# Scratch of rotated queries and keys, laid out by head and row first

## The chip, the cores and the metric

The kernel runs on one core of a Trainium2 chip. The metric is the device time of one execution in microseconds, as the median over runs. The core has a matrix engine (TensorE, PE in the profile; its weight loads are a row of their own, PEld), a vector engine (VectorE, DVE), a scalar engine (ScalarE, ACT), a third elementwise engine (GpSimd, POOL) and SyncE (SP), which here only issues transfers. Sixteen DMA engines move data between the device memory (DRAM) and the on-chip memory of 128 partitions. Matrix products accumulate in PSUM.

## What is computed

One layer of a streaming encoder over 2048 frames of width 1024, in float32. Only the part in bold passes through the changed code; the rest is the work around it.

```
h = rms_norm(x, norm_gain)
q_a, k_a, v_a, g_a, q_r, k_r, v_r, g_r, m_a, m_r = split(h @ w_in)
o_a = chunk_band_attention(q_a, k_a, v_a, rel_bias)            # 8 heads of 64
branch_a = (o_a * silu(g_a)) @ w_out_attn
qr, kr = rotary(q_r), rotary(k_r)                              # 8 heads of 64 = 2 halves of 32
o_r = retention_chunkwise(qr, kr, v_r)                         # keys 64, values 128
branch_r = (groupnorm(o_r) * silu(g_r)) @ w_out_ret
out = rms_norm(x + (sigmoid(m_a)*branch_a + sigmoid(m_r)*branch_r) @ w_out, final_gain)
```

**The rotation and the retention** are what matters. `rotary` takes the first and the second 32 columns of each head, `x1` and `x2`, and gives `x1*cos - x2*sin` and `x1*sin + x2*cos`. Retention forms products of queries and keys over the 64 columns of a head, weights them with a decay, multiplies by the values, and adds the query times a running state (the decayed sum of key times value of all earlier frames). A sum over the 64 columns does not depend on their order, provided queries, keys and state agree on it.

## The kernel before, in words

Every float32 operand of a matrix product is kept as a high and a low part (`split`: a rounded copy on ACT, the rest by a subtraction on DVE or POOL), and a product is made of two or three matrix products of parts. The 2048 frames are four blocks of `B` = 512 frames, and a block is two units of `T` = 256.

The program is written in stages: the projections to q, k, v of blocks 0 and 1 (`p0`), then attention and retention on them, the projections of blocks 2 and 3 (`p1`), attention and retention on these, then the output products. The gate projections (`g0`, `g1`) and part of the output products (`ba`, `br`) are a stream of dense steps that `fill(n)` interleaves with attention and retention: PE gets some retention matmuls, then some steps of dense matmuls (three matmuls of 512 columns each), and so on, in a written order that PE keeps. `later` and `put` hang DVE, POOL and DMA work on the count of those steps. All transfers except one are issued by SP (`dma`), in the order in which the program writes them. In attention and retention ACT, DVE and POOL are put in order by a scheduler, PE and SP are not.

**From projection to retention.** `ep_rotated` rotates the two halves of a group of four heads (`cc` is the group, 0 or 1). `xs[0]` and `xs[1]` are tiles of 128 rows, row = 32 * head in group + frequency: `xs[0]` has the first halves, `xs[1]` the second halves of all four heads. `parted` splits both and stores high and low parts to scratch in DRAM, `qrscr` (line 171) for queries and `krscr` (line 170) for keys, each 256 KB store taking 128 rows of two units of 256 frames. `keys` (line 896) also turns the rotated keys by 8 PE transposes a group and block (`trkr`), 64 in all, makes the high and low parts, and stores them to `kdscr`, from which the state is formed.

**Retention.** `retention(s, ...)` runs over pairs (`p`, `st`): four pairs of heads, and four units of 256 frames for each. There are 16 pairs in a stage, each of two items `i` (one head). `load(p, st)` (line 1276) brings what a pair needs: the keys `ks` (`kr`) by two transfers, the queries of each head (`qr`) by two transfers a head, values (`vr`) by one a head, the turned keys `kd` by one. A query tile has 128 partitions: the 64 columns of the head (two halves of 32) twice over, since high and low keys both meet the same queries. A key tile has the 64 high rows above the 64 low rows. `scores` makes four matmuls of 256 columns into `sr` from `kr` and `qr`, DVE multiplies by the decay mask (line 1326), ACT and DVE split the result into `sh` and `sl`. `output` makes six matmuls with the values, and two with the state where there is one, into `o`; `update` makes four matmuls `kv` from `vr` and `kd`. `evacuate` copies `o` (ACT, line 1383), stores it, squares it on POOL (line 1390), and splits the square for four `ssq` matmuls. The scores of an item are formed two items ahead of its output, and a pair is loaded when the item three ahead belongs to it, that is, its load is written one item before its first scores and a whole pair before its first output. Its tiles come from a ring of 21 buffers (`e`), so a load also waits until the tile that was in its buffer is read out.

The lines that the change touches read in this way in the kernel before. `r` is the row of the head within its group, 32 rows a head.

```
krscr[cc][b]: [unit, part, half, 128 rows, 256 frames]
qrscr[cc][b]: [unit, half, 128 rows, part, 256 frames]
ks[:, i]               <- krscr[un, :, :, r:r + 32]      "n h c t -> (n h) c t"
q[64*half:64*half+64]  <- qrscr[un, :, r:r + 32]         "h c n t -> h c (n t)"
```

Of the kernel before, what the change touches and what calls it, by code (L numbers as in the profile page):

```python
# [12 lines left out]
F32R = mybir.dt.float32r  # L13
# [8 lines left out]
P = 128  # L22
# [7 lines left out]
NB = SEQ // B  # L30
T = 256
# [34 lines left out]
def hybrid_kernel(  # L66
# [30 lines left out]
    def r32(ap):  # L97
        return ap.bitcast(F32)
# [7 lines left out]
    def E(name, dt=F32, shape=(P, 512)):  # L106
        return epool[0].tile(list(shape), dt, tag="e", name=name)

    def TR(name):
        return xpool[0].tile([P, 512], F32, tag="tr", name=name)  # L110

    def D(name, shape, dt=F32):
        return dram.tile(list(shape), dt, name=name)
# [31 lines left out]
    pe, act, dve, pool = Ordered(nc.tensor), Sometimes(nc.scalar), Sometimes(nc.vector), Sometimes(nc.gpsimd)  # L145
# [21 lines left out]
    kascr = [[D(f"kas_{h}_{b}", [P, B], F32R) for b in range(NB)] for h in range(HEADS)]  # L167
    vascr = [[D(f"vas_{h}_{b}", [P, B], F32R) for b in range(NB)] for h in range(HEADS)]

    krscr = [[D(f"krs_{c}_{b}", [2, 2, 2, P, T], F32R) for b in range(NB)] for c in range(2)]  # L170
    qrscr = [[D(f"qrs_{c}_{b}", [2, 2, P, 2, T], F32R) for b in range(NB)] for c in range(2)]
    kdscr = [[D(f"kds_{p}_{b}", [P, 2, 2, T], F32R) for b in range(NB)] for p in range(4)]
    vrscr = [[D(f"vrs_{h}_{b}", [P, 4, 2, DV], F32R) for b in range(NB)] for h in range(HEADS)]
    uascr = [[D(f"uas_{p}_{b}", [P, B]) for b in range(NB)] for p in range(4)]
# [59 lines left out]
    def later(n, fn):  # L234

        order[0] += 1
        deferred.append((steps[0] + n, order[0], fn))
        deferred.sort(key=lambda e: e[:2])

    def put(lag, dst, src):  # L240

        later(lag, lambda: dma(dst, src))
# [522 lines left out]
    def halves(t):  # L765
        return r32(t).rearrange("p (u n) -> p u n", u=2)

    def two(name, shape=(P, 512)):
        return [E(f"{n}_{name}", F32R, shape) for n in "hl"]
# [75 lines left out]
    def ep_rotated(kind):  # L845

        def epilogue(cc, b, j, src, ps):
            a = plain(src, ps, f"x{kind}_{cc}_{b}_{j}")
            if (kind, cc, b) not in firsts:
                firsts[kind, cc, b] = j, a  # L850
                return
            j0, a0 = firsts.pop((kind, cc, b))
            xs = [a, a0] if j0 else [a0, a]
            c, s = tables.pop((kind, cc, b))
            nm = f"{kind}_{cc}_{b}"
            ts = [E(f"t{n}_{nm}") for n in range(2)]

            def cross():
                for n in range(2):
                    pool.tensor_tensor(ts[n], xs[1 - n], s, ALU.mult)  # L860

            def own(n):
                dve.tensor_tensor(xs[n], xs[n], c, ALU.mult)

            def both(n):
                dve.tensor_tensor(xs[n], xs[n], ts[n], ALU.add if n else ALU.subtract)

            later(3, cross)
            for n in range(2):
                later(7 + n, lambda n=n: own(n))  # L870
                later(9 + n, lambda n=n: both(n))
            (keys if kind == "k" else queries)(cc, b, xs, nm)

        return epilogue

    def parted(xs, nm, at, eng, dst):

        ws = {}

        def high(n):  # L880
            ws[n] = two(f"{nm}_{n}")
            act.copy(ws[n][0], xs[n])

        def low(n):
            eng.tensor_tensor(ws[n][1], xs[n], r32(ws[n][0]), ALU.subtract)
            for i in range(2):
                put(4, dst(i, n), halves(ws[n][i]))

        for n in range(2):
            later(at + n, lambda n=n: high(n))  # L890
            later(at + 4 + 2 * n, lambda n=n: low(n))

    def queries(cc, b, xs, nm):
        parted(xs, nm, 13, dve, lambda i, h: r32(qrscr[cc][b][:, h, :, i, :]).rearrange("u r t -> r u t"))

    def keys(cc, b, xs, nm):
        parted(xs, nm, 13, pool, lambda i, h: r32(krscr[cc][b][:, i, h]).rearrange("u r t -> r u t"))

        def turn(u):
            pk = TR(f"trkr_{nm}_{u}")  # L900
            v = pk.rearrange("p (t i h c) -> p t h i c", t=2, i=4, h=2)
            for t in range(2):
                for h in range(2):
                    pe.transpose(v[:, t, h], xs[h][:, (2 * u + t) * P:(2 * u + t + 1) * P], ident)
            pk = pk.rearrange("p (t i d) -> p i t d", t=2, i=4)
            kt = []

            def high(n):
                kt.append(E(f"kdt_{nm}_{u}_{n}", F32R, (P, 2, 2, P)))
                act.copy(kt[n][:, :, :, 0:HD], pk[:, 2 * n:2 * n + 2])  # L910

            def low(n):
                dve.tensor_tensor(
                    kt[n][:, :, :, HD:P], pk[:, 2 * n:2 * n + 2], r32(kt[n][:, :, :, 0:HD]), ALU.subtract
                )
                put(4, r32(kdscr[2 * cc + n][b][:, u]), r32(kt[n]).rearrange("p i t c -> p i (t c)"))

            for n in range(2):
                later(2 + n, lambda n=n: high(n))
                later(5 + n, lambda n=n: low(n))  # L920

        for u in range(2):
            later(15 + 4 * u, lambda u=u: turn(u))
# [344 lines left out]
    def retention(s, ps_ret):  # L1268
# [8 lines left out]
        def load(p, st):  # L1277
            b, un = st // 2, st % 2
            nm = f"{p}_{st}"
            cc = p // 2  # L1280
            ks = E(f"kr_{nm}", F32R, (P, 2, T))
            qs, vs = [], []
            for i in range(2):
                r = 32 * (2 * (p % 2) + i)
                dma(
                    r32(ks[:, i]),
                    r32(krscr[cc][b][un, :, :, r:r + 32]).rearrange("n h c t -> (n h) c t"),
                )
            for i in range(2):
                r = 32 * (2 * (p % 2) + i)  # L1290
                q = E(f"qr_{nm}_{i}", F32R, (P, 2, T))
                for half in range(2):
                    dma(
                        r32(q[64 * half:64 * half + 64]).rearrange("d n t -> d (n t)"),
                        r32(qrscr[cc][b][un, :, r:r + 32]).rearrange("h c n t -> h c (n t)"),
                    )
                qs.append(q)
                v = E(f"vr_{nm}_{i}", F32R, (P, 2, 2 * DV))
                dma(
                    r32(v), r32(vrscr[2 * p + i][b][:, 2 * un:2 * un + 2]).rearrange("p t n d -> p t (n d)")  # L1300
                )
                vs.append(v)
            kd = E(f"kd_{nm}", F32R, (P, 2, T))
            dma(r32(kd), r32(kdscr[p][b][:, un]))
            tiles[p, st] = ks, qs, vs, kd.rearrange("p i (t c) -> p i t c", t=2)
            if st == 4:
                sstk = epool[0].tile([P, 2, DV], F32R, tag="sstk", bufs=2, name=f"sstk_{p}_{st}")
                dma(r32(sstk).rearrange("p i c -> p (i c)"), r32(skscr[p]))
                sstks[p, 4] = sstk
# [98 lines left out]

        load_masks(0)
        load(*todo[0])  # L1410
        load(*todo[1])
        pend = None
        items = [(p, st, i) for p, st in todo for i in range(2)]
# [5 lines left out]
        for n, (p, st, i) in enumerate(items):  # L1419
            if i == 0:  # L1420
                ops = ps_ret.tile([P, 512], F32, tag="o", bufs=1, name=f"o_{p}_{st}")
            if i == 0 and st < 7:
                update(p, st)
            fill(RET_FILL)
            output(p, st, i, parts.pop((p, st, i)), ops)
            if i == 0 and pend:
                pend()
                pend = None
            if i == 1:
                pend = evacuate(p, st, ops)  # L1430
                tiles.pop((p, st))
            if n + 2 < len(items):
                parts[items[n + 2]] = scores(*items[n + 2])
            if i == 1 and n + 3 < len(items):
                p2, st2, _ = items[n + 3]
                if st2 == 4 * s:
                    load_masks(p2)
                load(p2, st2)
            fill(RET_FILL)
# [186 lines left out]
```

## Time and profile before

| | us |
|---|---|
| median of 3 runs | 2388.63 |
| lowest and highest of them | 2388.27 and 2393.96 |
| the profiled execution | 2389.42 |
| its span, first to last instruction | 2387.6 |
| PE busy in the span | 2031.1 |
| DVE, ACT, POOL busy | 1424.5, 874.8, 794.7 |
| mean busy share of the DMA engines' largest queue | 56.8% |

The profile is that of one execution. Its span is 1.8 us shorter than its own time, and that time is 0.8 us above the median. A row of a view of waits names the engine and what it was about to do, then after the arrow what ended the wait, the total in microseconds, the number of waits and the longest. A row of a view of windows gives for a stretch of the span the busy time of each engine with its number of instructions, then the mean TensorE clock that was granted (1.00 is full), the mean busy share of the 16 DMA engines and the bytes per time that they moved. A row of the view by tile gives the shortest, the median and the longest of a group's instructions. The name `qr<-qrs` is a transfer from the scratch of the queries into a query tile.

The stages stand in the span as follows: `p0` up to about 370 us, attention to 615, retention of blocks 0 and 1 from 615 to 972, `p1` to about 1320, attention to 1612, retention of blocks 2 and 3 from 1612 to 2016, and the output products to the end.

### The profile page before, as it was taken

The page shows a single profiled execution, that of the slowest core. Times are in us where ns is not written, and L with a number is a line of the kernel's source. Part 1 is how long each engine was busy: PE and PEld are TensorE (multiplying, and loading weights), DVE is VectorE, ACT ScalarE, POOL GpSimd, SP SyncE. Part 2 cuts the span into 40 slices and gives each one's busy share as a digit, 9 for nine tenths or more (in the row PEclk, how much of TensorE's full clock was granted, in tenths as well). Part 3 has the DMA queues.
Part 4 walks back from the last instruction along what each step waited for, and adds up shares of the span by engine and source line. Part 5 has one row for each costly group of instructions (what it writes and reads, how often), then busy time and mean ns, then how long its engine had stood idle before and what let it go on. Part 6 is the DMA issues. An engine that isn't in the chain of part 4 may idle for free. (4 is left out here: it accounts for less than half of the span.)

```text
span 2387.6 us, 30310 instructions
## 1 busy us (share of the span) xinstructions
PE 2031.1 (85%) x9744; PEld 1675.8 (70%) x9744; DVE 1424.5 (60%) x2491; ACT 874.8 (37%) x1727; POOL 794.7 (33%) x868
## 2 busy tenths in 40 slices
PE   5899899999867665899999999996766558999998
PEld 4687678888645554777777888884655447788887
DVE  7868686776434435878876666653354345654554
ACT  5453334566322224333334555552232111122221
POOL 3645665444221123344445444432120012112000
PEclk9999999999878888899999999997878779999999
DMA  4476776454344446576666444434455655997654
GB/s 141 140 251 201 236 227 198 144 164 140 122 137 135 136 146 201 183 242 205 217 209 189 156 144 138 149 99 141 142 171 191 203 198 188 368 316 250 198 197 142
DMA packets 333391, 438.93 MB, mean 184 GB/s; under 512 B 27416, under 2 KB 190896, under 8 KB 333232
## 3 DMA queue, kind: packets, MB, share of 16 engines
q1 hardware_dynamic: 332192, 436.98, 56.8%
q8 instruction: 78, 1.28, 0.2%
q14 instruction: 81, 0.66, 0.1%
q10 hardware_dynamic: 1040, 0.00, 0.0%
HBM read 286.13 MB, written 150.76 MB: 183 GB/s over the span
## 5 line engine op out<-in xcount | busy, mean ns | idle before, releaser
L135 PE MATMUL sr<-qr,kr 128*128 128x256 f32 x256 | 58.5, 364 | 202.8 <-DMA qr<-qrs 96.5
L135 PEld LDWEIGHTS sr<-qr,kr 128*128 128x128 f32 x256 | 46.7, 253 | 214.0 <-DMA kd<-kds 121.0
L1326 DVE TENSOR_TENSOR sr<-sr,dm 128x512 f32<-128x512 f32 x64 | 44.7, 699 | 243.9 <-PE sr L135 243.5
L1180 POOL TENSOR_SCALAR pr<-pr,rsum 128x640 f32<-128x640 f32 (+4 forms) x128 | 97.2, 760 | 189.1 <-DVE rsum L1179 152.6
L135 PE MATMUL ps_g_x<-r,wh_g 128*128 128x512 f32 x448 | 151.3, 420 | 5.7 <-ACT wh_g L280 5.7
L135 PE MATMUL ps_g_z<-r,wh_g 128*128 128x512 f32 x448 | 150.5, 418 | 1.8 <-DVE u_g L344 1.3
L135 PE MATMUL ps_p_z<-r,wh_p 128*128 128x512 f32 x448 | 142.4, 399 | 8.3 <-DVE c_p L135 7.6
L135 PE MATMUL ps_p_x<-r,wh_p 128*128 128x512 f32 x448 | 144.2, 402 | 4.9 <-DVE r L135 4.8
L1178 ACT ACTIVATE pr<-pr,mn 128x640 f32<-128x640 f32 (+4 forms) x128 | 97.7, 763 | 114.4 <-DVE mn L1175 113.9
L1390 POOL TENSOR_TENSOR o<-oz 128x512 f32<-128x512 f32 x32 | 35.2, 1100 | 292.8 <-ACT oz L1383 257.7
L281 POOL TENSOR_TENSOR wl_g<-t_g,wh_g 128x512 fp32r<-128x512 f32 x52 | 67.7, 1301 | 187.0 <-ACT wh_g L280 183.0
L135 POOL TENSOR_TENSOR t_p<-raw_p,t_p 128x512 f32<-128x512 f32 x50 | 71.2, 1424 | 146.7 <-DVE wl_p L135 126.0
L207 DVE TENSOR_TENSOR ptl<-tp,pth 128x384 fp32r<-128x384 f32 x168 | 99.0, 598 | 35.0 <-ACT pth L206 32.1
L1065 POOL TENSOR_TENSOR gr<-gr,ta 128x512 f32<-128x512 f32 x32 | 47.3, 1477 | 209.9 <-DVE gr L1064 134.1
L1175 DVE CUSTOM_DVE_ANT_0 pr<-wide,bt 128x640 f32<-128x640 f32 (+4 forms) x128 | 94.2, 736 | 28.8 <-PE wide L135 26.4
L280 ACT CAST wh_g<-t_g 128x512 fp32r<-128x512 f32 x104 | 64.4, 621 | 118.5 <-PE ps_g_y L135 55.4
L135 PEld LDWEIGHTS ps_p_x<-r,wh_p 128*128 128x128 f32 x448 | 84.9, 193 | 24.0 <-DVE r L135 6.3
L206 ACT CAST sh<-sr 128x512 fp32r<-128x512 f32 x64 | 37.1, 582 | 174.4 <-DVE sr L1326 174.4
L135 PEld LDWEIGHTS ps_p_z<-r,wh_p 128*128 128x128 f32 x448 | 82.8, 190 | 25.4 <-issue 8.4
L135 DVE TENSOR_TENSOR wl_p<-t_p,wh_p 128x512 fp32r<-128x512 f32 x108 | 98.6, 913 | 0.5 <-ACT wh_p L135 0.4
L206 ACT CAST pth<-tp 128x384 fp32r<-128x384 f32 x168 | 84.2, 512 | 37.0 <-PE tp L135 30.3
L135 PE MATMUL wide<-ka,qa 128*128 128x512 f32 (+2 forms) x448 | 93.9, 326 | 2.2 <-DVE mn L1175 1.7
(1222 smaller groups left out, 6166.7 us busy)
## 6 DMA issues: line engine op xcount, KB each, us to landing
raw_g<-in_w_in_dram SPq DMA_DIRECT2D x56, 512.0 KB
raw_p<-in_w_in_dram SPq DMA_DIRECT2D x52, 512.0 KB
qa<-qas SPq DMA_DIRECT2D x128, 128.0 KB
qr<-qrs SPq DMA_DIRECT2D x128, 128.0 KB
vr<-vrs SPq DMA_DIRECT2D x64, 256.0 KB
ka<-kas SPq DMA_DIRECT2D x40, 256.0 KB
va<-vas SPq DMA_DIRECT2D x40, 256.0 KB
kds<-kdt_k SPq DMA_DIRECT2D x32, 256.0 KB
```

What stands on the lines that cost most here:

```text
L135: return tc.keep_in_program_order(op(*a, **k))
L206: act.copy(dst_h, src)
L207: (eng or dve).tensor_tensor(dst_l, src, r32(dst_h), ALU.subtract)
L280: act.copy(wh, src)
L281: soon(LO_LAG if strict[0] else 0, lambda: eng.tensor_tensor(wl, src, r32(wh), ALU.subtract))
L1065: pool.tensor_tensor(g, g, ta, ALU.add)
L1175: dve.tensor_tensor_reduce(pr[:, 0:w], sp, bts[h][:, WIN - w:WIN], 1.0, 3.0e38, ALU.add, ALU.min, mn,)
L1178: act.activation(pr[:, 0:w], pr[:, 0:w], AF.Exp, bias=mn, scale=-1.0, accum_out=rsum)
L1180: pool.tensor_scalar(pr[:, 0:w], pr[:, 0:w], rsum, 1.0, ALU.mult, ALU.mult)
L1326: dve.tensor_tensor(sp, sp, dms[p][i], ALU.mult)
L1390: pool.tensor_tensor(o2, oz, oz, ALU.mult)
```

## The change

The scratch of the rotated queries and keys gets another order of axes. A unit comes first, then for keys the part, then the head in the group, the frequency (32 of them), and inside a row the rotation half (and for queries the part). So the 64 columns of a head lie as 64 rows one after the other, frequency by frequency with both halves beside each other, where before the two halves lay 128 rows apart.

```
--- before
+++ after
@@ -167,8 +167,8 @@
-    krscr = [[D(f"krs_{c}_{b}", [2, 2, 2, P, T], F32R) for b in range(NB)] for c in range(2)]
-    qrscr = [[D(f"qrs_{c}_{b}", [2, 2, P, 2, T], F32R) for b in range(NB)] for c in range(2)]
+    krscr = [[D(f"krs_{c}_{b}", [2, 2, 4, 32, 2, T], F32R) for b in range(NB)] for c in range(2)]
+    qrscr = [[D(f"qrs_{c}_{b}", [2, 4, 32, 2, 2, T], F32R) for b in range(NB)] for c in range(2)]
@@ -891,14 +891,14 @@
     def queries(cc, b, xs, nm):
-        parted(xs, nm, 13, dve, lambda i, h: r32(qrscr[cc][b][:, h, :, i, :]).rearrange("u r t -> r u t"))
+        parted(xs, nm, 13, dve, lambda i, h: r32(qrscr[cc][b][:, :, :, h, i]).rearrange("u i c t -> (i c) u t"))
 
     def keys(cc, b, xs, nm):
-        parted(xs, nm, 13, pool, lambda i, h: r32(krscr[cc][b][:, i, h]).rearrange("u r t -> r u t"))
+        parted(xs, nm, 13, pool, lambda i, h: r32(krscr[cc][b][:, i, :, :, h]).rearrange("u i c t -> (i c) u t"))
 
         def turn(u):
             pk = TR(f"trkr_{nm}_{u}")
-            v = pk.rearrange("p (t i h c) -> p t h i c", t=2, i=4, h=2)
+            v = pk.rearrange("p (t i c h) -> p t h i c", t=2, i=4, h=2)
@@ -1280,19 +1280,17 @@
             ks = E(f"kr_{nm}", F32R, (P, 2, T))
             qs, vs = [], []
-            for i in range(2):
-                r = 32 * (2 * (p % 2) + i)
+            for n in range(2):
                 dma(
-                    r32(ks[:, i]),
-                    r32(krscr[cc][b][un, :, :, r:r + 32]).rearrange("n h c t -> (n h) c t"),
+                    r32(ks[64 * n:64 * n + 64]),
+                    r32(krscr[cc][b][un, n, 2 * (p % 2):2 * (p % 2) + 2]).rearrange("i c h t -> (c h) i t"),
                 )
             for i in range(2):
-                r = 32 * (2 * (p % 2) + i)
                 q = E(f"qr_{nm}_{i}", F32R, (P, 2, T))
                 for half in range(2):
                     dma(
-                        r32(q[64 * half:64 * half + 64]).rearrange("d n t -> d (n t)"),
-                        r32(qrscr[cc][b][un, :, r:r + 32]).rearrange("h c n t -> h c (n t)"),
+                        r32(q[64 * half:64 * half + 64]),
+                        r32(qrscr[cc][b][un, 2 * (p % 2) + i]).rearrange("c h n t -> (c h) n t"),
                     )
                 qs.append(q)
```

What each transfer walks through, outermost step first (counts of steps; the innermost run is in float32 elements and is contiguous):

| transfer | scratch side before | scratch side after | on-chip side before | on-chip side after |
|---|---|---|---|---|
| query load, 128 KB, 128 of them | 2 x 32 x 512 | 64 x 512 | 64 x 512 | 64 x 512 |
| key load, 128 KB, 64 of them | 4 x 32 x 256 | 64 x 2 x 256 | 128 x 256 | 64 x 2 x 256 |
| query store, 256 KB, 32 of them | 128 x 2 x 256, rows 2 KB apart | 128 x 2 x 256, rows 4 KB apart | 128 x 2 x 256 | the same |
| key store, 256 KB, 32 of them | 128 x 2 x 256, rows 1 KB apart | 128 x 2 x 256, rows 2 KB apart | 128 x 2 x 256 | the same |

The numbers of transfers, their bytes and the lengths of their contiguous runs stay. The PE, POOL and SP orders stay row for row; some shapes differ, and the lines behind the two that fall away are numbered two lower. At SP the first retention pairs read before:

```order
L135 DMA kr_0_6830<-krs_0_182 128x1x256 x2
L135 DMA qr_0_0_6833<-qrs_0_190 64x1x512 x2
L135 DMA vr_0_0_6836<-vrs_0_214 128x512
L135 DMA qr_0_1_6838<-qrs_0_190 64x1x512 x2
L135 DMA vr_0_1_6841<-vrs_0_218 128x512
L135 DMA kd_0_6843<-kds_0_198 128x512
```

and at the same place in the changed kernel, still on SP:

```order
L135 DMA kr_0_6830<-krs_0_182 64x2x256 x2
L135 DMA qr_0_0_6833<-qrs_0_190 64x512 x2
L135 DMA vr_0_0_6836<-vrs_0_214 128x512
L135 DMA qr_0_1_6838<-qrs_0_190 64x512 x2
L135 DMA vr_0_1_6841<-vrs_0_218 128x512
L135 DMA kd_0_6843<-kds_0_198 128x512
```

No transfer has moved. A key transfer brings one part of both heads where it brought both parts of one head.

The scheduler gives ACT and DVE another order at a few places in retention. The largest is at ACT in the first pairs of the first retention stage (`state`, `sh`, `sstk` belong to retention; `wh_g` and `u_g` to the interleaved gate projection). Before:

```order
L206 CAST sh_0_0_6929<-sr_0_0_6923 128x512
L280 CAST wh_g_8_3_7027<-raw_g_8_1_6662 128x512
L206 CAST sh_0_1_6948<-sr_0_1_6942 128x512
L339 COPY u_g_8_7007<-ps_g_8_x 128x512
L1358 CAST sstk_0_6997<-state 64x256
L206 CAST sh_1_0_7021<-sr_1_0_7015 128x512
```

and now, on ACT at the same place:

```order
L206 CAST sh_0_0_6929<-sr_0_0_6923 128x512
L339 COPY u_g_8_7007<-ps_g_8_x 128x512
L206 CAST sh_0_1_6948<-sr_0_1_6942 128x512
L1356 CAST sstk_0_6997<-state 64x256
L280 CAST wh_g_8_3_7027<-raw_g_8_1_6662 128x512
L206 CAST sh_1_0_7021<-sr_1_0_7015 128x512
```

The cast of one dense operand stands three rows later, the copy of a PSUM bank two rows earlier.

## The prediction

> **What bounds the kernel now.** I read the windows by stage first, since the page's mean of 85% for PE hides two stages that are unlike the rest.
>
> ```profile
> 615.00:972.00 357.00, 239.03 (x1100) 198.24 (x1099) 154.32 (x263) 107.99 (x201) 80.00 (x62) 0.83 0.47 154
> 1612.00:2016.00 404.00, 263.95 (x1193) 217.54 (x1192) 168.64 (x271) 93.52 (x170) 66.84 (x50) 0.79 0.54 177
> 340.00:615.00 275.00, 268.79 (x1487) 226.75 (x1486) 195.77 (x414) 153.31 (x333) 136.33 (x233) 1.00 0.54 167
> 972.00:1320.00 348.00, 326.25 (x1479) 264.37 (x1478) 262.03 (x373) 124.49 (x235) 154.84 (x121) 0.99 0.64 204
> 2016.00:2060.00 44.00, 37.15 (x147) 29.29 (x146) 35.45 (x51) 2.85 (x5) 9.39 (x6) 0.92 0.86 304
> ```
>
> The first two rows are the retention stages, the third an attention stage, the fourth a projection, the last the start of the output products. Outside retention PE is busy 94 to 98% of the time in rows three and four, at full clock. In retention no engine is busy: PE 67% and 65%, DVE 43% and 42%, and the granted clock falls to 0.83 and 0.79. The waits of PE in the two stages say for what:
>
> ```profile
> PE sr L135 <- DMA kd<-kds: 45.0, 8, 10.3
> PE sr L135 <- DMA qr<-qrs: 33.6, 6, 9.4
> PE sr L135 <- issue: 18.7, 4, 6.3
> PE o L135 <- ACT oz L1383: 9.2, 2, 4.8
> PE ssq L135 <- ACT o2h L206: 6.9, 3, 4.7
> PE ssq L135 <- DVE o2l L207: 3.6, 3, 2.5
> ...
> PE sr L135 <- DMA qr<-qrs: 62.9, 9, 11.6
> PE sr L135 <- DMA kd<-kds: 29.4, 5, 9.0
> PE o L135 <- ACT oz L1383: 19.1, 3, 11.3
> PE sr L135 <- issue: 13.0, 3, 6.7
> PE ssq L135 <- DVE o2l L207: 7.0, 6, 1.7
> PE ps_g_x L135 <- ACT wh_g L280: 5.7, 1, 5.7
> PE ssq L135 <- ACT o2h L206: 1.5, 2, 0.9
> ```
>
> The scores `sr` wait for their loads: 97.3 us in the first stage and 105.3 in the second. They read only `kr` and `qr`, so a releaser `kd`, or none shown ("issue"), is the tail of the same train of loads, and I count all three as one. The other rows are 19.7 and 33.3 us, for ACT and DVE.
>
> **Why the loads are late.** On the page the DMA engines are half idle while PE waits for them. The mean share is over 16 engines. The code gives a query load an outermost scratch step of 2 and a key load one of 4. Suppose that each goes through only so many engines. The sizes are
>
> ```profile
> qr<-qrs SPq DMA_DIRECT2D x128, 128.0 KB
> kr<-krs SPq DMA_DIRECT2D x64, 128.0 KB
> ```
>
> so a stage has 64 query loads (8.39 MB) and 32 key loads (4.19 MB). The first stage moved 357 us x 154 GB/s = 55.0 MB. An engine that takes half of the queries, a quarter of the keys and a sixteenth of the other 42.4 MB moves 4.19 + 1.05 + 2.65 = 7.89 MB, or 22.1 GB/s. In the second stage, of 71.5 MB, it is 4.19 + 1.05 + 3.68 = 8.92 MB in 404 us: again 22.1 GB/s. What a busy engine moves follows from the rows above: 154 / 16 / 0.47 = 20.5 GB/s, 177 / 16 / 0.54 = 20.5, 304 / 16 / 0.86 = 22.1. So under this supposition two engines are full from end to end in both stages, and the lengths of both stages come out of one number. That is my main reason. Spread over 16, the loads would ask for 9.6 and 11.1 GB/s of every engine, and nothing would be late. The issuing queue agrees:
>
> ```profile
> L135 SPq DMA_DIRECT2D qr<-qrs x128: 481/504/3404, 617.7 to 1978.5; - x128
> L135 SPq DMA_DIRECT2D vr<-vrs x64: 378/1962/3794, 618.8 to 1980.4; - x64
> L135 SPq DMA_DIRECT2D va<-vas x40: 325/374/452, 380.4 to 1570.3; - x40
> L135 SPq DMA_DIRECT2D qa<-qas x128: 444/587/1182, 381.8 to 1575.5; - x128
> ...
>   DMA qa<-qas: 0.5, 1
> ...
> SPq L135 <- DMA qr<-qrs: 45.4, 29, 2.7
> ```
>
> `vr` in retention and `va` in attention are transfers of one shape, 128 rows of 512; issuing `va` takes 374 ns, and `vr`, which stands behind query loads, 1962. SP itself is held up. And `qa` is what the changed query loads will look like (64 rows of 512 on both sides): in both attention stages together PE waits 0.5 us for it, once.
>
> [...]
>
> **The change, part by part.** *Query and key loads.* Their number, bytes and contiguous runs stay; each gets 64 outermost steps on both sides. What goes is first the three waits of `sr`, 97.3 + 105.3 = 202.6 us. Second, the slow clock behind them. PE at full speed needs 0.227 us for a matmul of 512 columns and 0.12 for one of 256:
>
> ```profile
> 2205.25 5.44 PE ps_out_(0, 0)_19999 L135 x24
> 1673.48 0.96 PE o L135 x8
> ```
>
> A stage has 496 matmuls of 256 columns by the code (128 for scores, 192 for outputs, 112 for states and their updates, 64 for `ssq`), and the windows count 1100 and 1193 in all, so 604 and 697 of 512 columns. At full speed that is 196.4 and 217.5 us. The first stage is 357 = 196.4 + 117.0 of waits + 43.6 of slowness; the second 404 = 217.5 + 138.6 + 47.9. What the slowness is can be seen around one wait:
>
> ```profile
> 621.87 0.39 PE L135 MATMUL ps_g_w<-r,wl_g 128*128 128x512 f32 x1
> 629.10 1.19 PE L135 MATMUL sr<-qr,kr 128*128 128x256 f32 x4 [6.84 <-DMA kd<-kds]
> 630.95 0.63 PE L135 MATMUL ps_g_w<-r,wl_g 128*128 128x512 f32 x1
> ```
>
> After 6.84 us of idleness the same matmul takes 0.63 instead of 0.39 for some microseconds. I give the load waits their part of it: 97.3/117.0 of 43.6 and 105.3/138.6 of 47.9, 36.3 + 36.4 = 72.7 us. Sum of the gain so far: 275 us.
>
> *What is late next.* With the loads in time PE reaches the outputs sooner, and ACT, DVE and POOL have about 135 us less a stage for the same work. Their waits above (19.7 + 33.3 us, with 19 us of slowness) could vanish, as in the attention row, where PE idles 6 us of 275 beside busier helpers; or double, 72 us more. DVE would be at 154/227, 68%, and in the projection row it is at 75% with PE at 94%. That row is the nearest, so I take 20 us, nearer to the low end.
>
> *Bandwidth.* Spread evenly the engines need 55.0 MB/16/20.5 GB/s = 168 us and 71.5/16/20.5 = 218 us of busy time. With stages of about 230 and 275 us that is 73% and 79%, between the shares of the last two windows.
>
> *SP.* The order and count of issues stay; a pair's nine loads at about 0.5 us (`qa`, `va` above) are 4.5 us of the pair's 14, hidden. Waiting for tiles of the ring stays as it is, since tiles come free by PE's progress.
>
> *Stores.* 64 stores of 256 KB have rows twice as far apart. They run in the projections, and nothing waits for them. As bounds: `ors` and `kds` stores with the same or wider steps stand there already, so from 0 to, at double their 0.8 us each (256 KB at 16 x 20.5 GB/s), 51 us of transfer time in two projections that by the fourth window are 348 us each and 64% used. I take 0.
>
> *Transposes.* 64 of them write PSUM with a step of two elements instead of runs of 32.
>
> ```profile
> L135 PE MATMUL trkr_k<-ident,u_p x32: 270/273/477, 116.0 to 1180.9; 128*128 128x128 f32 x32
> L135 PE MATMUL trva<-ident,u_p x32: 270/272/273, 135.1 to 1257.0; 128*128 128x128 f32 x32
> ```
>
> Runs of 32 cost nothing against the plain `trva`; at worst a step of two doubles them, 64 x 0.27 = 17 us, which I keep for the range and take as 0. The reordering at ACT and DVE moves casts of 0.6 us by two or three rows: 0.
>
> The sum: 2389.4 of the profiled execution - 275 + 20 = 2134. The median lies 0.8 below that execution, so **2133 us**.
>
> **Rivals.** *All 16 engines become the bound.* If retention cannot hold more than 0.71 of the DMA engines' time (between the shares 0.64 and 0.86 above), the stages are 168/0.71 = 237 and 218/0.71 = 307 us instead of 357 and 404, a gain of 217: 2172. For it speaks that the second stage also brings gates and weights for the output products; against it the 0.86. [...]
>
> *The helpers become the bound.* Each item then takes what ACT, POOL and DVE need one after the other between `o` and `ssq`. If their waits triple (106 us more, clock included 145), the time is 2389 - 275 + 145 = 2259. The DVE share of 68% speaks against.
>
> *The change does not spread the loads*, because they were spread already and something else makes them late: 2389. The two 22.1 would then be chance.
>
> *Slower: the stores.* If the wider row step made a store take 12 times its 0.8 us, the 64 would add 564 us of transfer time to projections that have about 36% of 2 x 348 = 250 us to spare; 314 us would come onto the path, more than the 255 gained: 2133 + 314 = 2447. It decides from about eleven times on. The waits show nothing of stores with 4 KB steps now.
>
> **How the numbers follow.** Chances: forecast 0.64 (own range 2080 to 2165), bandwidth 0.18, helpers 0.10, no spreading 0.04, slower 0.04. The range goes down to 2070, where nearly all other waits of retention (53 and 19 of slowness, from 2114) go for the most part too, and up to 2230, over the bandwidth case and toward the helpers'. A measurement of this kernel tells 0.3%, 7 us, from no change. Faster 0.93, same 0.03, slower 0.04.
>
> **What would show it.** Right: `sr` waits for loads under 30 us in all, `vr` issued in about 0.4 us, the retention windows near 230 and 275 us with clock above 0.93 and DMA share above 0.7, the other stages as before. Wrong: DMA share of 0.47 with `vr` still at 1.9 us (no spreading); `sr` waits with a share above 0.8 (bandwidth); long `o` and `ssq` waits for ACT (helpers); longer windows of the projections (stores, or `trkr` above 0.27 us).

## The result and the profile after

The changed kernel takes 2126.4 us (median of 4 runs, 2122.4 to 2129.0) against 2390.3 us (median of 4 runs). The ratio is 0.8893, 95% interval 0.8874 to 0.8912: 264 us less. The profiled execution took 2129.0 us with a span of 2127.2 us.

The windows of the changed kernel, cut where the first mask load of a retention stage is issued and where its last `ssq` is read. The columns are those of the prediction's windows: length, busy time of PE, PEld, DVE, ACT and POOL, granted clock, mean share of the 16 DMA engines, GB/s.

```profile
0.00:622.50 622.50, 563.10 (x2791) 463.21 (x2792) 456.29 (x779) 304.41 (x632) 320.05 (x368) 0.97 0.57 179
622.50:851.50 229.00, 207.93 (x1100) 177.42 (x1099) 154.94 (x263) 106.08 (x201) 79.77 (x62) 0.95 0.76 240
851.50:1484.60 633.10, 608.93 (x3091) 505.13 (x3090) 448.59 (x757) 287.40 (x565) 291.93 (x364) 0.99 0.55 174
1484.60:1754.00 269.40, 236.98 (x1218) 201.26 (x1217) 169.78 (x274) 96.22 (x174) 65.78 (x50) 0.92 0.84 270
1754.00:2127.20 373.20, 355.31 (x1551) 291.35 (x1549) 196.55 (x421) 79.20 (x157) 36.67 (x25) 0.99 0.72 240
```

The same cuts in the kernel before. Two of them lie a few microseconds from those of the prediction, so that both kernels have the same 1100 and 1218 PE instructions in a stage:

```profile
0.00:615.00 615.00, 559.17 (x2791) 459.24 (x2792) 454.48 (x779) 304.19 (x632) 321.07 (x368) 0.98 0.58 181
1607.00:2016.60 409.60, 269.55 (x1218) 222.20 (x1217) 170.71 (x274) 95.99 (x173) 66.84 (x50) 0.80 0.54 178
```

The first retention stage went from 357 to 229 us, the second from 409.6 to 269.4. That is 268 us, and the two profiled executions differ by 260. The difference is in the first row: the stretch before the first retention is 7.5 us longer. Most of that was there before any changed instruction ran (below).

What PE still waits for in the two stages of the changed kernel, the first five rows in the first stage, the others in the second:

```profile
PE sr L135 <- DMA qr<-qrs: 8.4, 5, 3.3
PE o L135 <- ACT oz L1381: 7.2, 2, 4.4
PE ssq L135 <- ACT o2h L206: 2.5, 2, 1.4
PE ssq L135 <- DVE o2l L207: 1.8, 2, 1.1
PE o L135 <- DVE sl L207: 1.2, 1, 1.2
...
PE o L135 <- ACT oz L1381: 16.6, 2, 9.1
PE sr L135 <- DMA qr<-qrs: 9.9, 4, 5.8
PE ssq L135 <- DVE o2l L207: 3.8, 5, 1.2
PE o L135 <- DVE sstk L1357: 1.2, 1, 1.2
PE sr L135 <- issue: 1.0, 1, 1.0
```

Waits of `sr` for loads fell from 202.6 to 19.3 us. The view by tile of the changed kernel shows the issuing queue nearly free again:

```profile
L135 SPq DMA_DIRECT2D qr<-qrs x128: 444/587/1267, 625.3 to 1725.3; - x128
L135 SPq DMA_DIRECT2D vr<-vrs x64: 325/534/1668, 626.6 to 1726.0; - x64
L135 SPq DMA_DIRECT2D kr<-krs x64: 593/606/928, 624.0 to 1721.6; - x64
```

A value load is issued in 0.53 us at the median instead of 1.96, against the 0.4 that the prediction named. Issuing a query load takes exactly what `qa` took, 587 ns. The clock of the second stage, 0.92, is just under the 0.93 that was named.

### The profile page after: what moved, and what is told of

It reads as the page before. It is cut to its first block, busy times and chain, and to the rows that moved or that the text cites. A ratio compares the mean times of both kernels' runs of the same rounds, so it can differ in the third digit from the quotient of the medians.

```text
span 2127.2 us, 30311 instructions
## 1 busy us (share of the span) xinstructions
PE 1972.2 (93%) x9744; PEld 1638.4 (77%) x9744; DVE 1426.2 (67%) x2491; ACT 873.3 (41%) x1727; POOL 794.2 (37%) x868
## 5 line engine op out<-in xcount | busy, mean ns | idle before, releaser
L135 PE MATMUL ps_g_z<-r,wh_g 128*128 128x512 f32 x448 | 144.9, 405 | 1.8 <-DVE u_g L344 1.3
L135 PE MATMUL ps_g_x<-r,wh_g 128*128 128x512 f32 x448 | 146.4, 408 | 0.0
L207 DVE TENSOR_TENSOR ptl<-tp,pth 128x384 fp32r<-128x384 f32 x168 | 98.9, 598 | 34.3 <-ACT pth L206 31.8
L135 PE MATMUL ps_p_x<-r,wl_p 128*128 128x512 f32 x224 | 90.2, 403 | 6.9 <-DVE wl_p L135 6.9
L135 PEld LDWEIGHTS tp<-ident,pr 128*128 128x128 f32 x560 | 70.2, 140 | 33.8 <-DVE ptl L207 10.3
L135 PE MATMUL tp<-ident,pr 128*128 128x128 f32 x560 | 89.2, 273 | 7.0 <-DVE ptl L207 6.5
L135 PE MATMUL ps_p_z<-r,wl_p 128*128 128x512 f32 x224 | 89.5, 399 | 0.4 <-DVE wl_p L135 0.4
L280 ACT CAST wh_g<-t_g 128x512 fp32r<-128x512 f32 x104 | 64.5, 621 | 61.2 <-PE ps_g_y L135 22.1
```

What stands on the lines that cost most here:

```text
L135: return tc.keep_in_program_order(op(*a, **k))
L207: (eng or dve).tensor_tensor(dst_l, src, r32(dst_h), ALU.subtract)
L280: act.copy(wh, src)
```

## The experiments

The theory is the supposition of the prediction: a load goes through only as many engines as it has outermost steps on the scratch side, 2 for a query load and 4 for a key load before, and through all 16 with the 64 steps after. Two engines would then have been full through both retention stages, with every other load queued behind them. The first rival is that the new place of the rows in DRAM, each load one contiguous piece, is what is faster. All ratios are to runs of the kernel before on the same chip (medians of 2389 to 2392 us).

**Old layout, queries spread by cutting.**

```
-                for half in range(2):
-                    dma(q[64*half:64*half+64], qrscr[cc][b][un, :, r:r + 32])   "h c n t -> h c (n t)"
+                for half in range(2):
+                    for h in range(2):
+                        dma(q[64*half+32*h:64*half+32*h+32], qrscr[cc][b][un, h, r:r + 32])
```

> The layout of before, each query load of 64 rows cut into its two halves of 32 rows (256 loads of 64 KB with 32 outermost steps instead of 128 of 128 KB with 2); keys as before (4 outermost steps). Theory of few engines: an engine with a quarter of the keys has 1.05 + 3.18 = 4.23 MB in the first retention stage and 1.05 + 4.21 = 5.26 MB in the second, 191 and 238 us at 22.1 GB/s, under the changed kernel's 229 and 269, so nearly the whole gain comes without the new layout: 2126 to 2155 us. Rival, the contiguous 128 KB of a load in the new layout are what is faster: 2389 us or a little more, since there are more transfers to issue.

Measured: 2187.8 us (ratio 0.9153, interval 0.9138 to 0.9168). 201 of the 264 us come without the new layout, so the layout rival falls. The time is 33 us above the end of my range, and the next runs look for what is missing.

**Old layout, only the keys spread.**

```
-            for i in range(2):
-                dma(ks[:, i], krscr[cc][b][un, :, :, r:r + 32])   "n h c t -> (n h) c t"
+            for n in range(2):
+                for h in range(2):
+                    dma(ks[64*n+32*h:64*n+32*h+32], krscr[cc][b][un, n, h, 64*(p%2):64*(p%2)+64])
```

> The layout of before, only the key loads cut so that they have 32 outermost steps (4 of 64 KB a pair instead of 2 of 128 KB); queries as before. Theory of few engines: the two engines of the queries keep 4.19 + 2.91 = 7.10 MB and 4.19 + 3.94 = 8.13 MB, 321 and 368 us at 22.1 GB/s instead of 357 and 404, so about 2317 us. Rival, the key loads are a small matter or the keys were not bound to few engines: 2389 us.

**New layout, queries on two engines again.**

```
-                        q[64*half:64*half+64] <- qrscr[un, 2*(p%2)+i]   "c h n t -> (c h) n t"
+                        q[64*half:64*half+64] <- qrscr[un, 2*(p%2)+i]   "c h n t -> h c (n t)"
-            v = pk.rearrange("p (t i c h) -> p t h i c", t=2, i=4, h=2)
+            v = pk.rearrange("p (t i h c) -> p t h i c", t=2, i=4, h=2)
...
(keys in four loads of 32 rows, as in the run above, but from the new scratch)
```

> The new layout of the scratch and its stores, but the query loads read it half by half, with 2 outermost steps again (rows of a head 4 KB apart within the same contiguous 128 KB); the key loads are cut into 4 of 32 outermost steps, the turned keys in the order of before. Theory of few engines: 7.10 and 8.13 MB on two engines again, 321 and 368 us at 22.1 GB/s, so about 2317 us. Rival, the place of the rows in DRAM decides: near the changed kernel, 2126 to 2160 us.

Measured: 2350.5 us (ratio 0.9838, 0.9819 to 0.9858) and 2348.8 us (0.9831, 0.9812 to 0.9851). The two agree, although one has the old and the other the new scratch. With the same bytes in the same contiguous 128 KB, two outermost steps for the queries bring back nearly the old time: in these runs the number of steps decides, not the place. The size is off: 2317 was expected. The windows of the run with the new layout and two steps:

```profile
619.50:955.00 335.50, 241.83 (x1098) 200.78 (x1097) 154.19 (x263) 107.94 (x201) 80.50 (x61) 0.82 0.52 164
1589.20:1976.00 386.80, 266.80 (x1218) 220.08 (x1217) 169.52 (x275) 96.29 (x173) 66.69 (x50) 0.81 0.59 188
```

By the count of the prediction the two engines now carry 7.10 MB in the first and 4.19 + 4.02 = 8.21 MB in the second of these windows (which moved 72.7 MB), that is 21.2 GB/s in both, 4% less than the 22.1 of the kernel before. Whether they had small gaps, or the cut key loads cost them more time for their bytes, these runs do not separate.

**The loads alone.** A kernel of nothing but loads gives the cost of a transfer by its shape.

```
+    for n, (ap, shape, alternate) in enumerate([...twelve patterns...]):
+        for j in range(16):
+            dma(big[p0:p0 + p, j, 0:f], w_in at j * 1 MB, walked by ap)
+        one or two DVE copies that read the first element of all 16
```

> Nothing of the layer is computed: twelve stretches of 16 loads of an input, one after the other, each stretch ended by one or two copies on DVE that read all 16; then zeros are written. Stretches of 2.1 MB with 2, 4, 8, 16 and 64 outermost steps on 64 rows; 64 again, alternating between the two halves of the partitions; the key load before (4 steps on 128 rows of 1 KB, 2.1 MB); the key load after on one half, then alternating; then 4.2 MB each of 128 rows of 2 KB, of 64 rows of 4 KB on one half, and of these alternating. Theory of few engines: 2 steps 47 us, 4 steps 24, 8 steps 12 (at 22.1 GB/s an engine and 2 us of latency), 16 and 64 steps about 8 to 9 us, the time of 16 issues of 0.5 us; the key load 24 us before and 9 after. Rival, every transfer goes over all engines: about 9 us in all of these. [...]

Its windows, one a stretch in the order of the expectation. This kernel uses neither PE nor ACT, so a row has DVE and POOL, then the clock, the mean share of the 16 engines and GB/s:

```profile
0.00:45.20 45.20, 0.08 (x1) 1.41 (x6) 1.00 0.12 46
45.20:68.90 23.70, 0.11 (x2) 0.00 (x0) 1.00 0.24 88
68.90:84.80 15.90, 0.14 (x1) 0.00 (x0) 1.00 0.42 132
84.80:97.30 12.50, 0.17 (x1) 0.00 (x0) 1.00 0.58 168
97.30:110.30 13.00, 0.19 (x2) 0.00 (x0) 1.00 0.56 162
110.30:122.70 12.40, 0.36 (x3) 0.00 (x0) 1.00 0.59 169
122.70:147.10 24.40, 0.12 (x1) 0.00 (x0) 1.00 0.25 86
147.10:160.10 13.00, 0.21 (x2) 0.00 (x0) 1.00 0.54 161
...
172.80:186.10 13.30, 0.09 (x2) 0.00 (x0) 1.00 0.90 315
186.10:208.70 22.60, 0.17 (x1) 0.00 (x0) 1.00 0.90 186
208.70:229.60 20.90, 0.38 (x3) 0.00 (x0) 1.00 0.95 226
```

The share fits the supposed count of engines: 0.12 is 2 of 16, 0.24 and 0.25 are 4 of 16. With 8 and 16 steps the 0.42 and 0.58 lie below the 0.50 and 1.00 of such a count; what limits there, these rows do not tell. The 2 us of latency in the expectation are near the shortest time from issue to landing that the changed kernel's views by tile give, 2.1 us (`qrs`, `krs`); the medians there are 3.4 and 3.2 us. The old query load (first row) moves 46 GB/s, 23 an engine if two move it; the old key load (seventh) 86. From 2 steps to 64 the time falls from 45 to 13 us, not to the 8 or 9 expected, but far from the equal times of the rival.

The last rows set 64 rows of one half beside 128. 128 rows of 2 KB move 315 GB/s, and the same 4.2 MB as 64 rows of 4 KB on one half of the partitions 186, with the engines busy 0.90 of the time in both. So these transfers to 64 rows of one half, back to back, keep the engines busy 1.7 times as long for their bytes. The stretches of 64 rows of 2 KB run at 161 to 169 GB/s, near the 186, but the price in busy time is smaller: 13.0 us x 0.56 = 7.3 us for 2.1 MB, against 6.0 for the same bytes in 128 rows. In the last row the halves alternate; the stores at the end of this kernel begin inside it, so its 226 GB/s is not that of the loads, which is 4.2 MB in 20.9 us, 201 GB/s. Why 64 rows of one half cost the engines more, these runs do not show.

**What the queries-only run lacked.** Two runs tell the keys with four steps from the price of cutting: the old layout with both cut, and the changed kernel with only its query loads cut.

```
+  old layout: query loads and key loads both of 32 rows, as in the first two runs together
```

> The layout of before, query and key loads both cut to 32 outermost steps. The run with only the queries cut ended 61 us above the changed kernel. Theory A, these 61 us are the keys on four engines: 2126 to 2145 us. Theory B, they are the price of twice as many transfers of 64 KB on 32 rows: 2185 us or more, since now the keys pay it too.

```
-                    dma(q[64*half:64*half+64], qrscr[cc][b][un, 2*(p%2)+i])
+                    for c0 in (0, 16):
+                        dma(q[64*half+2*c0:64*half+2*c0+32], qrscr[cc][b][un, 2*(p%2)+i, c0:c0+16])
```

> The changed kernel, each query load of 64 rows cut into two of 32 consecutive rows (256 loads of 64 KB); nothing else. Theory A (keys on four engines were the shortfall of the old layout with cut queries): 2126 to 2140 us. Theory B (the price of small transfers): 2170 to 2190 us.

Measured: 2146.8 us (ratio 0.8983, 0.8954 to 0.9012) and 2143.7 us (0.8970, 0.8941 to 0.8998). Both theories hold in part: spreading the keys too is worth 41 us (2187.8 to 2146.8), and cutting 128 query loads into 256 costs 17 us (2126.4 to 2143.7). The two runs are 3 us apart, within their intervals, although the first has the old layout and cuts the keys too; and the two runs with queries on two steps, old and new layout, were 2 us apart. So no gain of the layout as such shows; what it gives is a spread without more transfers. The gains of the two spreads nearly add up, 201 of the queries and 38 of the keys, to the 244 of both.

The 41 us of the keys are more than the theory of full engines allows. The first retention stage of the queries-only run reads

```profile
618.90:874.30 255.40, 216.24 (x1098) 182.66 (x1097) 155.55 (x264) 107.21 (x201) 77.05 (x61) 0.91 0.69 214
```

and an engine with a quarter of the keys carried 4.23 MB in these 255.4 us by the same count, 16.6 GB/s and not 22. By that count it was not full, and the keys with four steps still cost time. How, these runs do not show.

**Can what is left be had?** Three more runs tried to beat the changed kernel.

```
-RET_FILLS = (2.7, 3.3)
+RET_FILLS = (2.7, 3.7)
```

> The changed kernel with 3.7 instead of 3.3 dense steps at each place of the second retention stage (some 27 steps of 0.68 us move there from the output products). What is left there of PE waits (33 us) and of the slow clock are gaps that more dense work between scores and outputs can cover: 2115 to 2124 us. Rival, the stage is held by the DMA engines, busy 0.84 of it, and the moved steps bring their weight loads with them: 2126 us, no change.

Measured: 2124.6 us, ratio 0.8886 (0.8863 to 0.8910). That cannot be told from 0.8893, as the rival had it. The second retention stage grew from 269 to 288.5 us and the output products shrank from 373 to 355: the moved steps cost as much time in the one place as in the other.

```
-    qrscr = [... [2, 4, 32, 2, 2, T] ...]
+    qrscr = [... [2, 4, 2, 32, 2, 2, T] ...]          # each head's 64 rows twice, one after the other
-    one store of 128 rows a tile
+    eight stores of 32 rows a tile (four heads, two copies)
-                for half in range(2):
-                    dma(q[64*half:64*half+64], qrscr[cc][b][un, 2*(p%2)+i])
+                dma(q, qrscr[cc][b][un, 2*(p%2)+i])   # 128 rows
```

> The changed kernel, with each query row stored twice, the two copies of a head side by side, by stores of 32 rows (256 of 64 KB instead of 32 of 256 KB), so that a query tile is loaded by one transfer of 128 rows (64 of 256 KB instead of 128 of 128 KB). The loads alone took 0.78 us per 128 KB on 64 rows and 0.83 us per 256 KB on 128 rows. If the 64-row loads cost retention something, 32 x 0.73 = 23 us of DMA time fall away in each stage, and with them most of the 19 us of score waits and some slow clock: 2100 to 2115 us. Rival, the 224 additional issues (0.4 us each on SP) and 8 MB in the projections cost as much or more: 2126 to 2160 us.

Measured: 2162.1 us, ratio 0.9046 (0.9021 to 0.9071), slower than the changed kernel. Its windows show a gain and a larger loss:

```profile
0.00:650.10 650.10, 564.74 (x2793) 463.62 (x2794) 456.47 (x779) 304.46 (x633) 319.37 (x368) 0.96 0.58 178
650.10:863.50 213.40, 202.25 (x1097) 174.39 (x1096) 154.49 (x264) 106.08 (x201) 79.44 (x61) 0.96 0.80 255
863.50:1524.00 660.50, 615.41 (x3094) 509.37 (x3092) 450.18 (x756) 287.04 (x565) 293.90 (x365) 0.97 0.56 174
1524.00:1784.50 260.50, 235.22 (x1221) 199.77 (x1220) 170.19 (x276) 96.26 (x173) 66.30 (x50) 0.95 0.84 280
```

Retention takes 213 and 260 us where the changed kernel takes 229 and 269. So the 64-row query loads, or their number, do hold it back, by some 24 us in all (this run halves the number as well). But the two stretches with projections are 27 us longer each. PE's waits for `pst`, behind POOL (25.0 us), and for `trvr`, behind ACT (28.6 us), went from 5.5 to 53.6 us in all, which is about the loss. By the program that work of POOL and ACT needs loaded inputs and weights; that late loads hold it up is an estimate. The next run spread the eight stores of a tile two dense steps apart:

```
-                for rows, to in d:
-                    put(4, to, halves(ws[n][i])[rows])
+                for m, (rows, to) in enumerate(d):
+                    put(4 + 2 * m, to, halves(ws[n][i])[rows])
```

> The run with queries stored twice, with the eight 64 KB stores of each tile two dense steps apart instead of all at once. That run had retention stages of 212 and 259 us (227 and 269 in the changed kernel) and lost 27 us in each of the two stretches with projections. If the bursts of 32 stores hold up SP and the loads behind them, spreading gives back most of the 54 us: 2100 to 2115 us. Rival, the tiles that are held longer, or the number of issues itself, cost as much: 2140 us or more.

Measured: 2162.6 us, ratio 0.9047 (0.9030 to 0.9064). Spread in this way the stores cost as much, so the bursts are not the cause. Whether the number of issues or the tiles held longer cost the time stays open.

**Two queues for the two halves.** Loads to the upper 64 partitions come from ACT here, those to the lower from SP. I expected up to the 15 and 10 us that the loads of 128 rows brought in the two retention stages: 2100 to 2120 us.

```
-                dma(ks[64*n:64*n+64], ...)
+                (act.dma_start if n else dma)(ks[64*n:64*n+64], ...)
-                    dma(q[64*half:64*half+64], ...)
+                    (act.dma_start if half else dma)(q[64*half:64*half+64], ...)
```

> The changed kernel, with the loads of the upper 64 partitions of keys and queries (96 of 192) issued by ACT instead of SP. [...] Rival, ACT is held up by its own issues and by waiting for free tiles: 2126 to 2160 us.

Measured: 2174.3 us, ratio 0.9094 (0.9069 to 0.9118), the rival's side and beyond its range. Beside it ran a second kernel of loads alone:

```
+        nine patterns of 16 loads; (nc.scalar if two and j % 2 else nc.sync).dma_start(...)
```

> Nothing of the layer is computed, as in the other run of loads alone. Nine stretches of 16 loads: 64 rows of 2 KB on one half from SP (12.5 us as measured); the same from SP and ACT in turn; the same alternating the halves, one half from each queue; 128 rows of 2 KB from SP (13.2 us as measured for 4.2 MB); the same from both; 64 rows of 4 KB on one half from both queues; the same alternating; 32 rows of 2 KB from SP; the same from both. [...] If the limit is the time of an issue (0.5 us) or a fixed cost of each transfer, two queues speed up one half as well, to about 7 us. 32 rows: 8 us from SP if issues decide, about 12 if a transfer has a fixed cost of 0.75 us.

Its timeline on DVE: each copy ends a stretch, and the bracket is about the time since the copy before. The first four rows are 64 rows of 2 KB on one half from SP, from both queues, with alternating halves from both queues, and 128 rows from SP. The next two are 64 rows of 4 KB, both queues, on one half and with the halves alternating; the last two 32 rows of 2 KB, from SP and from both:

```profile
13.19 0.17 DVE L95 COPY got<-big 64x16 f32<-64x16 f32 x1 [13.19 <-DMA big<-in_w_in_dram]
26.04 0.17 DVE L95 COPY got<-big 64x16 f32<-64x16 f32 x1 [12.69 <-DMA big<-in_w_in_dram]
34.65 0.36 DVE L93 COPY got<-big 64x8 f32<-64x8 f32 x2 [8.44 <-DMA big<-in_w_in_dram]
49.35 0.17 DVE L95 COPY got<-big 128x16 f32<-128x16 f32 x1 [14.34 <-DMA big<-in_w_in_dram]
...
86.12 0.17 DVE L95 COPY got<-big 64x16 f32<-64x16 f32 x1 [22.96 <-DMA big<-in_w_in_dram]
105.11 0.36 DVE L93 COPY got<-big 64x8 f32<-64x8 f32 x2 [18.82 <-DMA big<-in_w_in_dram]
114.23 0.17 DVE L95 COPY got<-big 32x16 f32<-32x16 f32 x1 [8.76 <-DMA big<-in_w_in_dram]
121.95 0.16 DVE L95 COPY got<-big 32x16 f32<-32x16 f32 x1 [7.55 <-DMA big<-in_w_in_dram]
```

The 8.4 us of the third row are not the whole time of its loads, since that stretch had a head start. Its upper half is not what the copy before it reads, so ACT ran on into it:

```profile
13.38 15.53 ACTq L79 DMA_DIRECT2D big<-in_w_in_dram  x16
```

Five of the eight loads that ACT issues for the third stretch went out between 22.2 and 25.9 us, before the second ended at 26.04. The windows of the two stretches show the rates:

```profile
13.20:26.04 12.84, 0.15 (x1) 0.00 (x0) 1.00 0.93 190
26.04:34.65 8.61, 0.17 (x2) 0.00 (x0) 1.00 0.73 204
```

Together the two moved their 4.2 MB in 21.5 us, 196 GB/s, where from SP alone the same two kinds of stretch took 13.0 and 12.4 us. The two stretches of 4 KB rows overlap in the same way: 8.4 MB in 42.1 us, 199 GB/s, against 22.6 and 20.9 us. So two queues save 15% and 3% of the time and reach nothing near the 315 GB/s of 128 rows. That the two halves run beside each other is not shown. The 32 rows take 8.8 us from SP, near the 8 of issues alone and not the 12 of a fixed cost of each transfer.

In the kernel the loads of ACT moreover come late. The waits of PE in that kernel:

```profile
PE sr L135 <- DMA qr<-qrs: 58.5, 26, 5.0
```

58.5 us instead of 18.3. ACT issues its half of a query tile 3.2 us after SP issues the other, at the median of the 64 tiles; in the changed kernel the second half follows after 0.5 us. By the program ACT issues its loads between its casts and copies. That the waits of these are what delays the loads is argued from the program, not measured apart.

## Why the prediction was right

*What bounded the kernel.* That the few steps of the loads made them late is shown, by the cut loads, the two-step loads and the loads alone. That few engines were full fits most of it, not the 41 us of the keys: with two steps the loads alone have a mean share of 0.12, that of 2 engines of 16, and 23 GB/s for each of two, near the 22.1 that came out of both stages. No row names the engines of a transfer. The traces also count the signals that tell of a landing. For 16 loads of 2, 4, 8 and 16 steps the loads alone have 48, 80, 144 and 256 of them: 3, 5, 9 and 16 a load. In the first retention stage the kernel before has 2784 and the changed one 3968, for the same 247 transfers. The difference, 1184, is 64 x (16 - 3) for the query loads and 32 x (16 - 5) for the key loads, and it is 1184 in the second stage too. So the loads of the kernel before landed with as few signals as the loads of 2 and 4 steps do, and those of the changed kernel with as many as loads of 16. What one signal stands for, no run shows.

*The waits of the scores.* I let all 202.6 us go; 183.3 went, and 19.3 are left. In the run with queries loaded by 128 rows 6.9 are left, so most of it goes with the 64-row loads or with their number.

*The slow clock.* With 196.4 and 223.2 us of PE work at full speed in the two windows (the second has 722 matmuls of 512 columns by the count 1218), slowness was 91.4 us before (43.6 and 47.8) and is 25.2 now: 229.0 - 196.4 - 21.1 = 11.5 and 269.4 - 223.2 - 32.5 = 13.7. That is 66 us gained, where I had 72.7.

*What is late next.* This term had the wrong sign: I took 20 us more of waits for ACT, DVE and POOL. They fell, from 53.0 to 34.3 us (the 53.0 leave out two short DVE rows, 0.7 and 1.3, which the 47.8 and 43.6 of slowness contain). ACT's own waits for loads in the two stages fell too, from 50.2 to 30.4 us, which may be why; no run tests it. The sum is 183.3 + 66.2 + 18.7 = 268 us against the 255 forecast. That these are so near is partly luck: the three terms were off by 19, 7 and 39 us, and the last had the other sign.

*Bandwidth.* 73% and 79% were forecast, 76% and 84% measured. The first is off because a busy engine moved 240 / 16 / 0.76 = 19.7 GB/s instead of 20.5. The second has three small causes: 20.1 GB/s instead of 20.5, a stage of 269 us instead of 275, and a window with 72.7 MB instead of 71.5. So within the kernel a busy engine moved only 2 to 4% less than before; the 1.7 times of the loads alone does not show there. A sign of the bandwidth rival, a share above 0.8 with waits of `sr`, is met in part by the second stage (0.84 and 10.9 us), but the stage ended at 269 us and not at 307.

*Stores and transposes.* Both were taken as 0. The transposes with a step of two:

```profile
L135 PE MATMUL trkr_k<-ident,u_p x32: 270/273/421, 120.3 to 1059.8; 128*128 128x128 f32 x32
```

273 ns as before. The stretch between the retentions, which holds the second projection with its stores, went from 636.3 to 634.8 us from the last `ssq` of one stage to the first mask load of the next, and the output products behind the last read of `ssq` from 371.7 to 373.5 us.

*What was not forecast.* The opening stretch is 7.5 us longer in the profiled execution, and 4.4 us of that were there at the first key store, the first changed transfer:

```profile
L135 SPq DMA_DIRECT2D krs<-h_k x16: 367/446/700, 116.6 to 1184.0; - x16
```

```profile
L135 SPq DMA_DIRECT2D krs<-h_k x16: 366/445/688, 121.0 to 1064.3; - x16
```

(kernel before, then the changed one). Among the other runs the first mask load is issued between 616.6 and 622.4 us, with the old layout and with the new, apart from the two that store the queries twice; one run with the old layout has its first key store at 120.8 us. So I take it as chance of the start, without a run that shows it; the profiled execution is also the slowest of its four. The 8 us lost here and the 13 us gained above make up the distance between the 2129 of the profiled execution and the 2134 that the prediction's sum gave for it.

*The rivals.* No spreading and slower stores are excluded. Helpers as the bound did not happen: DVE is busy 68% and 63% of the two stages, and PE waits for it 3.0 and 5.0 us.

## What to carry to other kernels

A mean share of the DMA engines near one half (0.47 and 0.54 here) with a compute engine waiting for loads (202.6 us) can mean that a few engines are full: add up the bytes by the outermost count of each access pattern and compare two stages of different length. Lay scratch out so that a load has many outermost steps (16 loads of 128 KB alone took 45.2 us with 2 steps, 23.7 with 4, 15.9 with 8, 12.5 with 16 and 13.0 with 64) without cutting the load; cutting gave 92% of the same gain (244 of 264 us). When a stretch of loads is timed alone, look whether loads of the next stretch begin inside it.

## What the hardware showed that I had not expected

Back to back, loads to 64 partitions of one half cost the engines 1.7 times as long for their bytes (186 against 315 GB/s at the same share of 0.90). Alternating the halves changed that little, from one queue (201 GB/s) and from two (199). Cutting 128 KB loads into 64 KB ones cost 17 us for 128 additional transfers. Key loads of four outermost steps cost 41 us although four engines with a quarter of them each were not full by the count (16.6 GB/s against 22.1). Gains in one stage were eaten by another: retention 24 us shorter, with queries stored twice, came with 54 us in the projections.
